# A hybrid diffusion block on one core: retention norm without a mean, states decayed on GpSimd, tiles reordered

## The chip, the cores and the metric

The kernel runs on one core of one Trainium2 chip. The metric is the device time of one execution in microseconds (us). Its engines are TensorE (PE; its weight loads are PEld), VectorE (DVE), ScalarE (ACT), GpSimd (POOL) and SyncE (SP), each with an instruction queue of its own that it works through in order; 16 DMA engines move data.

## The reference

One layer over 1024 latent tokens and 256 context tokens, model width 1024, four gated-DeltaNet heads and four retention heads of 128. What the change touches is the retention group: `r_f` and `r_b` are chunkwise retentions in the two directions, with a state R that is decayed by a constant of the head and chunk, and the norm of their sum subtracts the mean of each head.

```python
def head_group_norm(t, g):
    mu = jnp.mean(t, axis=-1, keepdims=True)
    var = jnp.mean(jnp.square(t - mu), axis=-1, keepdims=True)
    return (t - mu) * lax.rsqrt(var + NORM_EPS) * g.astype(jnp.float32)
...
    def step(S, xs):                      # gated delta rule, per chunk
        u_c, w_c, q_c, qk_c, k_c, gl = xs
        v_new = u_c - jnp.einsum('bhck,bhkv->bhcv', w_c, S)
        o = jnp.einsum('bhck,bhkv->bhcv', q_c, S) + jnp.einsum('bhij,bhjv->bhiv', qk_c, v_new)
        S = gl * S + jnp.einsum('bhck,bhcv->bhkv', k_c, v_new)
        return S, o
...
    def step(R, xs):                      # retention, per chunk
        q_c, k_c, v_c = xs
        o = jnp.einsum('bhik,bhkv->bhiv', q_c * xi[..., None], R)
        R = g_chunk * R + jnp.einsum('bhjk,bhjv->bhkv', k_c * zeta[..., None], v_c)
        return R, o
...
    o_ret = head_group_norm(r_f + r_b, ret_norm_g) * jax.nn.silu(rg...)
    y = jnp.concatenate([o_gdn, o_ret], axis=-1)
    x = x + g1 * (y[:, CTX_LEN:] @ w_out)
```

The output of a retention head is linear in v, and v = h @ w_v: a mean over the 128 columns of a head's output is zero if the mean over these columns has been taken out of the value weights.

## The kernel before

The kernel is written as one program, and a list scheduler decides the order of the instructions on each engine; within an engine they run in that order. A tile of tokens has 128 rows; there are ten, two of context (0, 1) and eight of latent tokens (`LAT`). The span falls into stages:

- To about 86 us: adaLN and the norm. `xt` are loaded token tiles, `junk` their squares, `rx2s`, `rx3s` the square roots of two groups of tiles (four latent ones, two context ones), `xtr` the transposes on TensorE, and `hhi`, `hlo` the modulated result as a high and a low part (L233 to L236).
- Projections. `token_major` (L326) multiplies 128 tokens by 256 columns of weights, in 24 matmuls into a PSUM tile `tm` (L335 to L337); a finishing instruction writes `res`, which goes to DRAM (`rd` for the groups rv, rk, rq, rg, `zd` for z). `fin_copy` (L357) is a Copy on ScalarE, `fin_gate` (L360) a Silu. Weights are split in a high part on ScalarE (`whi`, L279) and a low part (`wlo`, L280). Groups 0 and 1 are rv, 2 and 3 rk, 4 and 5 rq, 6 and 7 rg. The convolutions for k, q and v stand between them.
- The chunk solve of the delta rule, to about 620 us.
- The scan, to 726 us: `step` (L737) in both directions side by side, a state `S` each, with products `kS`, `Tr`, `up`, `o`; beside it the backward retention states `Rb` (`backward`, by `rstate`, L857), for which `kz` is made on GpSimd from a loaded `pk`. `gate` (L796) norms and gates the delta output `O` into `yo`, with `zg` loaded for it.
- Retention, forward (`forward`, L884), with its last four steps from 722 to 762 us: `rqT`, `rkT` (transposes), `qk` (copies on ScalarE and two products with the decays `XI`), `rP` (the product of k and q), `pm` (masked, on VectorE), `ro` (the output), then the norm and the gate, and `ru` for the next state `Rf`. All of `rqT`, `rkT`, `rP`, `ro`, `ru` share the PSUM banks of `bank_a`.
- Output projection (`op`): tiles of y are loaded in the order `pairs` (L1072), transposed (`yT`, L1003), split (`yhi`, `ylo`) and multiplied by `wohi`, `wolo`, which come from `woraw`. Then the FFN and its output (`ffn`, `fo`), to the end.

Square roots of the norms are taken in `rsqrt_mean`: a Sqrt on ScalarE and four or five small instructions on VectorE (`rrx` to `rry` for retention, `rgs` to `rgy` for the delta norm).

## Time and profile before

| | us |
|---|---|
| median of three runs | 1544.87 (1543.34 to 1545.88) |
| the profiled execution, its time | 1540.2 |
| the profiled execution, its span | 1538.3 |
| PE busy | 1440.2 (94%) |
| DVE busy | 988.5 (64%) |
| ACT busy | 621.9 (40%) |
| POOL busy | 644.0 (42%) |

The rows further down come from the profiled execution. Its span begins with its first instruction; start times are counted from there. The granted clock of a stretch is the mean over it, 1.00 for 2.4 GHz and 0.50 for 1.2 GHz.

### The profile page before, as it was taken

The page shows a single profiled execution, that of the slowest core. Times are in us where ns is not written, and L with a number is a line of the kernel's source. Part 1 is how long each engine was busy: PE and PEld are TensorE (multiplying, and loading weights), DVE is VectorE, ACT ScalarE, POOL GpSimd, SP SyncE. Part 2 cuts the span into 40 slices and gives each one's busy share as a digit, 9 for nine tenths or more (in the row PEclk, how much of TensorE's full clock was granted, in tenths as well). Part 3 has the DMA queues.
Part 4 walks back from the last instruction along what each step waited for, and adds up shares of the span by engine and source line. Part 5 has one row for each costly group of instructions (what it writes and reads, how often), then busy time and mean ns, then how long its engine had stood idle before and what let it go on. Part 6 is the DMA issues. An engine that isn't in the chain of part 4 may idle for free.

```text
span 1538.3 us, 24370 instructions
## 1 busy us (share of the span) xinstructions
PE 1440.2 (94%) x8973; PEld 1247.3 (81%) x8973; DVE 988.5 (64%) x1945; ACT 621.9 (40%) x1277; POOL 644.0 (42%) x594
## 2 busy tenths in 40 slices
PE   4799999988989999999799899996999999999997
PEld 1698887987989899999678688875888888888886
DVE  5855679389766634778847776753555555658477
ACT  5743455456451111334534443222333333355444
POOL 2310001476113332224407669987555554226321
PEclk9899999999989999999899999998999999999999
DMA  7554577587585565996743247576222221585862
GB/s 269 188 200 144 155 231 228 159 253 241 165 239 150 176 201 179 354 399 207 260 149 117 110 151 241 204 258 227 103 103 103 103 105 73 190 308 187 291 221 110
DMA packets 156486, 298.15 MB, mean 194 GB/s; under 512 B 43384, under 2 KB 75464, under 8 KB 150992
## 3 DMA queue, kind: packets, MB, share of 16 engines
q1 hardware_dynamic: 116624, 246.88, 47.5%
q10 hardware_dynamic: 36944, 41.08, 8.4%
q0 software_dynamic: 2800, 8.65, 1.6%
q8 instruction: 70, 1.15, 0.3%
q14 instruction: 48, 0.39, 0.1%
HBM read 206.60 MB, written 89.96 MB: 193 GB/s over the span
## 4 chain that ended last, share of the span: by engine, by line
PE 55%; POOL 8%; DMA 8%; DVE 7%; issue 3%; ACT 3%; SPq 0%; ACTq 0%; POOLq 0%; DVEq 0%
PE ffn L1158 6%; PE ffn L1156 6%; PE ffn L1157 6%; PE fo L1281 4%; PE fo L1283 4%; PE fo L1282 4%; PE tm L336 3%; PE tm L337 3%; PE tm L335 3%; DMA wd<-tw 2%; PE op L1018 1%; PE op L1017 1%; PE op L1019 1%; DMA sd<-sp 1%; POOL e L567 1%
## 5 line engine op out<-in xcount | busy, mean ns | idle before, releaser
L336 PE MATMUL tm<-wlo,hhi 128*128 128x256 f32 x704 | 205.8, 294 | 4.9 <-DVE wlo L280 4.9
L335 PE MATMUL tm<-whi,hhi 128*128 128x256 f32 x704 | 203.5, 293 | 5.4 <-ACT whi L279 3.0
L337 PE MATMUL tm<-whi,hlo 128*128 128x256 f32 x704 | 204.3, 293 | 0.0
L336 PEld LDWEIGHTS tm<-wlo,hhi 128*128 128x128 f32 x704 | 139.4, 198 | 7.6 <-DVE wlo L280 5.9
L335 PEld LDWEIGHTS tm<-whi,hhi 128*128 128x128 f32 x704 | 138.1, 198 | 7.6 <-ACT whi L279 3.7
L337 PEld LDWEIGHTS tm<-whi,hlo 128*128 128x128 f32 x704 | 139.2, 199 | 0.5 <-POOL hlo L236 0.2
L1156 PE MATMUL ffn<-t,whi 128*128 128x512 f32 x352 | 136.7, 389 | 1.1 <-ACT whi L279 1.1
L1158 PE MATMUL ffn<-t,wlo 128*128 128x512 f32 x352 | 136.9, 390 | 0.4 <-DVE wlo L280 0.4
L1157 PE MATMUL ffn<-t,whi 128*128 128x512 f32 x352 | 137.0, 389 | 0.0
L279 ACT ACTIVATE whi<-wraw 128x512 fp32r<-128x512 f32 (+1 forms) x98 | 75.2, 772 | 129.3 <-PE ffn L1157 84.5
L279 ACT ACTIVATE whi<-ws 128x512 fp32r<-128x512 f32 x88 | 55.6, 632 | 169.8 <-PE ffn L1157 134.8
L280 DVE TENSOR_TENSOR wlo<-ws,whi 128x512 fp32r<-128x512 f32 x88 | 91.4, 1039 | 46.5 <-ACT whi L279 46.4
L1156 PE MATMUL ffn<-b,whi 128*128 128x512 f32 x264 | 104.8, 397 | 16.5 <-ACT whi L279 16.5
L1282 PE MATMUL fo<-wlo,ahi 128*128 128x512 f32 x308 | 119.8, 389 | 0.0
L1281 PE MATMUL fo<-whi,ahi 128*128 128x512 f32 x308 | 119.3, 389 | 0.1
L1283 PE MATMUL fo<-whi,alo 128*128 128x512 f32 x308 | 119.0, 389 | 0.0
L280 DVE TENSOR_TENSOR wlo<-wraw,whi 128x512 fp32r<-128x512 f32 (+1 forms) x92 | 99.0, 1078 | 20.0 <-ACT whi L279 20.0
L1158 PE MATMUL ffn<-b,wlo 128*128 128x512 f32 x264 | 104.6, 396 | 1.9 <-DVE wlo L280 1.9
L1157 PE MATMUL ffn<-b,whi 128*128 128x512 f32 x264 | 104.6, 396 | 0.0
L280 DVE TENSOR_TENSOR wlo<-raw,whi 128x512 fp32r<-128x512 f32 x77 | 66.6, 890 | 52.1 <-ACT whi L279 52.1
L460 PE MATMUL b<-hhi,whi 128*128 128x512 f32 (+1 forms) x256 | 94.3, 368 | 0.3 <-ACT y L464 0.3
L461 PE MATMUL b<-hlo,whi 128*128 128x512 f32 (+1 forms) x256 | 94.1, 368 | 0.0
(430 smaller groups left out, 3638.1 us busy)
## 6 DMA issues: line engine op xcount, KB each, us to landing
adaw<-ada_w SPq DMA_DIRECT2D x48, 512.0 KB, 4.8
pk<-sd SPq DMA_DIRECT2D x16, 1536.0 KB, 7.8
wraw<-wfi SPq DMA_DIRECT2D x44, 512.0 KB, 3.5
ar<-ad SPq DMA_DIRECT2D x33, 512.0 KB, 4.4
w<-wfo SPq DMA_DIRECT2D x22, 512.0 KB, 5.3
wd<-tw SPq DMA_DIRECT2D x11, 1024.0 KB, 4.8
ad<-act SPq DMA_DIRECT2D x20, 512.0 KB, 3.0
raw<-wd SPq DMA_DIRECT2D x20, 512.0 KB, 6.5
```

Source lines behind the costliest of these rows:

```text
L279: S.activation(hi, raw, AF.Copy)
L280: e.tensor_tensor(lo, raw, hi.bitcast(F32), ALU.subtract)
L335: T.matmul(o, hhi[:, k, tsl], whi[:, k % 4, :], start=(k == 0), stop=False)
L336: T.matmul(o, hhi[:, k, tsl], wlo[:, k % 4, :], start=False, stop=False)
L337: T.matmul(o, hlo[:, k, tsl], whi[:, k % 4, :], start=False, stop=(k == KT - 1))
L460: T.matmul(o, whi[:, k, :], hh, start=(k == 0), stop=False)
L1156: T.matmul(o, whi[:, k, :], xhi(xn, slice(0, 4), k), start=(first and k == 0), stop=False, **kw)
L1157: T.matmul(o, whi[:, k, :], xlo(xn, slice(0, 4), k), start=False, stop=False, **kw)
L1158: T.matmul(o, wlo[:, k, :], xhi(xn, slice(0, 4), k), start=False, stop=(k == 3), **kw)
L1281: T.matmul(po[g][i], ahi[:, ts], whi, start=(j == 0 and not kw), stop=False, **kw)
L1282: T.matmul(po[g][i], ahi[:, ts], wlo, start=False, stop=False, **kw)
L1283: T.matmul(po[g][i], alo[:, ts], whi, start=False, stop=(j == FH - 1), **kw)
```

## The change

Six things change.

1. The value weights (groups 0 and 1) are centred on chip by head: the sum over each 128 columns, times -1/128, is added to them. The retention output then has no mean, and the norm needs only its mean square.
2. rg is projected in the place of rv, and rv in that of rg.
3. In `forward` the evacuation of `ro`, `bn_stats`, `bn_aggr`, `nm` and the Identity go; four Squares read `ro` in PSUM and accumulate `ss`, and four scalar_tensor_tensors take `ro` from PSUM, the root and the gate to `oc`. One of the two `XI` products moves from GpSimd to VectorE, which reads `rqT` in PSUM, and the twelve `ro` matmuls go by operand instead of by head.
4. The old states are multiplied by their decay on GpSimd (`aged`), ahead of the product that they are added to; VectorE then adds 512 columns at once.
5. `zg` has two buffers instead of one, in another pool.
6. Tiles go into `op` in another order.

```diff
+            if center:
+                n = shape[0] * shape[1] // P
+                heads = raw.rearrange("p k (h j) -> p (k h) j", j=P)
+                mean = R1.tile([P, n], F32, tag="mean", name="mean")
+                V.tensor_reduce(mean, heads, axis=AX.X, op=ALU.add)
+                V.scalar_tensor_tensor(heads, bc(mean, [P, n, P], 2), -1.0 / P, heads, ALU.mult, ALU.add)
...
-        for g in range(2):
-            token_major(g, ALL, fin_copy, S, W, SY, last_ada)
-            ada_rest(2, g)
+        for g in (6, 7):
+            token_major(g, LAT, fin_gate, S, W, SY, last_ada)
+            ada_rest(2, g % 2)
...
-        for g in (6, 7):
-            token_major(g, LAT, fin_gate, S, W2, SY)
+        for g in range(2):
+            token_major(g, ALL, fin_copy, S, W2, SY)
...
+            aged = None
+            if old is not None and not last and RTS:
+                aged = RTS[0].tile([P, H, P], F32, tag="aged%d" % d, name="aged%d" % d, bufs=1)
+                G.tensor_tensor(aged, old, bc(sm["gl"][:, c8(t, d)], [P, H, P], 2), ALU.mult)
...
+                elif aged is not None:
+                    V.tensor_tensor(ns.rearrange("p h v -> p (h v)"), pu, aged.rearrange("p h v -> p (h v)"), ALU.add)
...
-            zg = load(SC, zd[l], "zg", 1, (P, 512))
+            zg = load(RTS[0], zd[l], "zg", 2, (P, 512))
...
+            if prev is not None:
+                aged = RT.tile([P, H, P], F32, tag="aged", name="aged", bufs=2)
+                G.tensor_tensor(aged, prev, bc(gch[:, 4 * d:4 * d + 4], [P, H, P], 2), ALU.mult)
...
-                for h in range(H):
-                    V.scalar_tensor_tensor(ns[:, h, :], prev[:, h, :], gch[:, 4 * d + h:4 * d + h + 1],
-                                           pu[:, h * P:(h + 1) * P], ALU.mult, ALU.add)
+                V.tensor_tensor(ns.rearrange("p h v -> p (h v)"), pu, aged.rearrange("p h v -> p (h v)"), ALU.add)
...
-                for d in range(2):
-                    G.tensor_tensor(qk[:, 2 + d], qk[:, 0], XI[d], ALU.mult)
+                V.tensor_tensor(qk[:, 2], pq.rearrange("p (h i) -> p h i", i=P), XI[0], ALU.mult)
+                G.tensor_tensor(qk[:, 3], qk[:, 0], XI[1], ALU.mult)
...
+                for h in range(H):
+                    T.matmul(po[:, hsl[h]], qk[:, 2, h, :], cur[:, h, :], start=(h == 0), stop=(h == 0),
+                             skip_group_check=h > 0)
+                for h in range(H):
+                    T.matmul(po[:, hsl[h]], pm[:, h, :], vv[:, hsl[h]], start=False, stop=False, skip_group_check=True)
+                for h in range(H):
+                    T.matmul(po[:, hsl[h]], qk[:, 3, h, :], rb[t][:, h, :], start=False, stop=True,
+                             skip_group_check=True)
...
+                for h in range(H):
+                    S.activation(oc[:, h, :], po[:, h * P:(h + 1) * P], AF.Square, accum_out=ss[:, h:h + 1])
+                rs = rsqrt_mean(RT, ss, H, "rr", P)
...
-                S.activation(oc.rearrange("p h v -> p (h v)"), po, AF.Copy)
...
-                for h in range(H):
-                    V.bn_stats(bst[:, h, :], oc[:, h, :])
-                for h in range(H):
-                    V.bn_aggr(mv[:, h, :], bst[:, h, :])
-                rs = rsqrt_mean(RT, mv[:, :, 1], H, "rr", 1.0)
...
-                for h in range(H):
-                    S.activation(oc[:, h, :], oc[:, h, :], AF.Identity,
-                                 bias=nm_[:, h:h + 1], scale=rs[:, h:h + 1])
-                yf = oc.rearrange("p h v -> p (h v)")
-                G.tensor_tensor(yf, yf, gt, ALU.mult)
+                    V.scalar_tensor_tensor(oc[:, h, :], po[:, hs], rs[:, h:h + 1], gt[:, hs], ALU.mult, ALU.mult)
...
-        pairs = (0, 4, 1, 5, 2, 6, 3, 7)
-        nxt = op_y(0)
+        pairs = (1, 5, 2, 6, 0, 4, 3, 7)
+        nxt = op_y(1)
```

The scheduler moves instructions. The first place is ScalarE at the front, between the squares of the two context tiles and the modulation of the four latent tiles `hhi` (- is before, + the changed kernel; its lines are some numbers higher, so L357 answers to L368 and L342 to L350).

```order
 L247 ACTIVATE junk,ms<-xt 128x1024 x2
-L357 ACTIVATE res<-tm 128x256
+L368 ACT_TABLE_LOAD
+L368 ACTIVATE res<-tm 128x256
+L125 ACT_TABLE_LOAD
 L125 ACTIVATE rx3s<-ms,epsb 128x2
-L357 ACTIVATE res<-tm 128x256
-L342 DMA rd<-res 128x256 x2
+L368 ACT_TABLE_LOAD
+L368 ACTIVATE res<-tm 128x256
+L350 DMA rd<-res 128x256 x2
 L233 ACTIVATE hhi<-xtr,bmix,amix 128x512 x8
```

Three table loads now stand between the squares and `hhi`; two more stand a few rows earlier, one ahead of the two `res` that come before the first DMA `xt<-ctx`, one ahead of `rx2s`, which comes before the second.

The second place is GpSimd in the scan rounds. Before, the twelve `kz` of the backward states stand there without anything between them.

```order
L354 TENSOR_TENSOR res<-ra,res 128x2x64 x2
L342 DMA rd<-res 128x256
L859 TENSOR_TENSOR kz<-pk,Z 128x512 x12
L898 TENSOR_TENSOR qk<-qk,XI_7004 128x512
L898 TENSOR_TENSOR qk<-qk,XI_7005 128x512
```

In the changed kernel `aged` of the backward states (L876, numbered `Rb`) and of the scan states (L764, `S`) stand between them.

```order
L878 TENSOR_TENSOR kz<-pk,Z 128x512 x3
L876 TENSOR_TENSOR aged<-Rf,gch 128x512
L876 TENSOR_TENSOR aged<-Rb_7147,gch 128x512
L764 TENSOR_TENSOR aged_7279<-S_7209,gl 128x512
L876 TENSOR_TENSOR aged<-Rb_7160,gch 128x512
L764 TENSOR_TENSOR aged_7293<-S_7216,gl 128x512
L878 TENSOR_TENSOR kz<-pk,Z 128x512 x3
L876 TENSOR_TENSOR aged<-Rb_7249,gch 128x512
L876 TENSOR_TENSOR aged<-Rb_7262,gch 128x512
L764 TENSOR_TENSOR aged_7394<-S_7324,gl 128x512
L876 TENSOR_TENSOR aged<-Rb_7275,gch 128x512
L764 TENSOR_TENSOR aged_7408<-S_7331,gl 128x512
```

A round now has three `kz`, three or two `aged` of Rb and two of S, in this order.

The third place is VectorE in the last retention steps. Before, a step's rows there are these: statistics of the step ahead, a group of `yo`, the mask `pm`, the root's small instructions, the four state updates in two pieces.

```order
L915 BN_STATS bst<-oc 128x6 x2
L807 SCALAR_TENSOR_TENSOR yo<-O,rgy,zg 128x128 x4
L915 BN_STATS bst<-oc 128x6 x2
L917 BN_AGGR mv<-bst 128x2 x4
L903 TENSOR_TENSOR pm<-rP,M 128x512
L127 TENSOR_SCALAR rrx<-mv 128x4
L132 RECIPROCAL rry<-rrs 128x4
L136 SCALAR_TENSOR_TENSOR rru<-rry,rrx 128x4
L137 TENSOR_TENSOR rru<-rru,rry 128x4
L138 SCALAR_TENSOR_TENSOR rry<-rru,rry 128x4
L869 SCALAR_TENSOR_TENSOR Rf<-Rf,gch,ru 128x128 x3
L920 SCALAR_TENSOR_TENSOR nm<-mv,rry 128x4
```

In the changed kernel the last steps read so; L939 is the gating of `ro` from PSUM, L914 the XI product, L920 is `pm`, L887 the state's add.

```order
L939 SCALAR_TENSOR_TENSOR oc<-ro,rry,pk 128x128 x4
L887 TENSOR_TENSOR Rf<-ru,aged 128x512
L127 TENSOR_SCALAR rrx<-ss 128x4
L132 RECIPROCAL rry<-rrs 128x4
L136 SCALAR_TENSOR_TENSOR rru<-rry,rrx 128x4
L914 TENSOR_TENSOR qk<-rqT,XI_7016 128x512
L137 TENSOR_TENSOR rru<-rru,rry 128x4
L138 SCALAR_TENSOR_TENSOR rry<-rru,rry 128x4
L939 SCALAR_TENSOR_TENSOR oc<-ro,rry,pk 128x128 x4
L920 TENSOR_TENSOR pm<-rP,M 128x512
L887 TENSOR_TENSOR Rf<-ru,aged 128x512
L1001 SCALAR_TENSOR_TENSOR wolo<-hf,gain,wohi 128x512 x3
```

The last `yo` stand ahead of these rows now, and a gating of the step ahead stands between the XI product and `pm`.

## Rows read from the trace of the kernel before

**Rows 1.** Windows: stretch, length, busy PE PEld DVE ACT POOL, clock, DMA share, GB/s.

```profile
84.00:620.00 536.00, 512.41 (x4263) 470.66 (x4262) 343.48 (x736) 210.42 (x481) 150.05 (x234) 0.96 0.64 198
650.00:675.00 25.00, 25.00 (x224) 24.91 (x224) 16.78 (x61) 6.54 (x17) 6.43 (x7) 1.00 1.00 390
722.00:762.20 40.20, 30.45 (x215) 28.62 (x213) 33.53 (x113) 21.89 (x65) 19.48 (x18) 0.87 0.80 275
775.00:800.00 25.00, 22.69 (x103) 17.34 (x102) 12.68 (x20) 8.65 (x14) 0.00 (x0) 1.00 0.34 114
```

**Rows 2.** Timeline of ScalarE: start, length (us), line, form, [idle before <-releaser].

```profile
60.37 0.41 ACTq L186 DMA_DIRECT2D xt<-ctx  x1
...
65.29 1.06 ACT L247 ACTIVATE junk<-xt 128x1024 f32<-128x1024 f32 x1 [0.83 <-DMA xt<-ctx]
...
67.61 2.12 ACT L233 ACTIVATE hhi<-xtr,bmix,amix 128x512 fp32r<-128x512 f32 x3 [0.44 <-PE xtr L258]
```

**Rows 3.** Timeline of TensorE at the front: the two waits for the modulated tiles.

```profile
68.44 0.38 PE L335 MATMUL tm<-whi,hhi 128*128 128x256 f32 x1 [1.09 <-ACT hhi L233]
...
69.91 1.37 PE L258 MATMUL xtr<-ident,xt 128*128 128x128 f32 x8 [0.49 <-DVE hf L235]
```

**Rows 4.** Groups by line on ScalarE, whole span: the table loads of the gate.

```profile
L360 ACT ACT_TABLE_LOAD x8 | 10.3, 1283 | 3.5 <-DMA zd<-res 2.9 <-ACT vt L704 0.4
```

**Rows 5.** Timeline of ScalarE at a table load and the instruction behind it.

```profile
93.55 1.28 ACT L419 ACT_TABLE_LOAD   x1
94.84 0.21 ACT L419 ACTIVATE nA<-alog 128x8 f32<-128x8 f32 x1
```

**Rows 6.** Timeline of GpSimd in the scan rounds: kz, and what it waited for.

```profile
645.43 1.04 POOL L859 TENSOR_TENSOR kz<-pk,Z 128x512 f32<-128x512 f32 x1 [6.36 <-DMA pk<-rd]
...
649.68 1.04 POOL L859 TENSOR_TENSOR kz<-pk,Z 128x512 f32<-128x512 f32 x1 [1.67 <-PE ru L863]
657.58 1.04 POOL L859 TENSOR_TENSOR kz<-pk,Z 128x512 f32<-128x512 f32 x1 [6.86 <-DMA pk<-rd]
```

**Rows 7.** Timeline of VectorE in the same round: the S update.

```profile
654.26 1.12 DVE L778 SCALAR_TENSOR_TENSOR S<-S,gl,up 128x128 f32<-128x128 f32 x4
```

**Rows 8.** Waits of TensorE, 722 to 768: us in total, times, longest us.

```profile
PE ro L909 <- DVE pm L903: 4.1, 3, 2.6
PE rP L901 <- ACT qk L896: 3.9, 3, 2.0
...
PE rqT L893 <- DMA pk<-rd: 0.8, 1, 0.8
```

**Rows 9.** Timeline of VectorE in the tail: what stands ahead of pm.

```profile
725.39 2.93 DVE L807 SCALAR_TENSOR_TENSOR yo<-O,rgy,zg 128x128 f32<-128x128 f32 x4 [1.12 <-DMA zg<-zd]
...
745.54 3.40 DVE L807 SCALAR_TENSOR_TENSOR yo<-O,rgy,zg 128x128 f32<-128x128 f32 x4
...
755.66 2.65 DVE L127 TENSOR_SCALAR rrx<-mv 128x4 f32<-128x4 f32 x1
```

**Rows 10.** Timeline of GpSimd in the tail: the qk products beside them.

```profile
745.92 2.60 POOL L898 TENSOR_TENSOR qk<-qk,XI 128x512 f32<-128x512 f32 x2
...
755.77 2.50 POOL L898 TENSOR_TENSOR qk<-qk,XI 128x512 f32<-128x512 f32 x2
```

**Rows 11.** Groups by line on VectorE, 620 to 765: mean ns of one is the last figure.

```profile
L869 DVE SCALAR_TENSOR_TENSOR Rf<-Rf,gch,ru 128x128 f32<-128x128 f32 x32 | 9.1, 340 | 0.4 <-PE ru L863 0.4
...
L915 DVE BATCH_NORM_STATS2 bst<-oc 128x6 f32<-128x128 f32 x31 | 6.9, 279 | 7.0 <-ACT oc L911 6.9
```

**Rows 12.** Groups by line on ScalarE, 620 to 765: the squares of the gate.

```profile
L802 ACT ACTIVATE yo<-O 128x128 f32<-128x128 f32 x32 | 9.5, 297 | 9.2 <-DVE O L792 6.1 <-DMA dy<-yo 3.0
```

**Rows 13.** Timeline of TensorE: last retention step, its last ro, first op matmul.

```profile
753.60 0.27 PE L893 MATMUL rqT<-ident,pk 128*128 128x128 f32 x1
...
761.73 0.39 PE L909 MATMUL ro<-pk,pm 128*128 128x128 f32 x2
...
766.83 0.80 PE L1017 MATMUL op<-wohi,yhi 128*128 128x512 f32 x1 [3.32 <-ACT yhi L1006]
```

More of the change, by code (lines that the diff above doesn't have):

```diff
@@ L312, in ada_rest, with weights @@
                     V.scalar_tensor_tensor(o, o, 1.0, gffn[:, ks], ALU.add, ALU.mult)
-        def weights(src, shape, e, pl, q=S, after=None):
+        def weights(src, shape, e, pl, q=S, after=None, center=False):
             raw = pl.tile([P] + shape, F32, tag="wraw", name="wraw")
@@ L326, in token_major @@
         def token_major(g, tiles, finish, store, pl, q=S, after=None):
-            w = [weights(ap["wt"][g, :, 4 * kh:4 * kh + 4, :], [4, 256], V, pl, q, after) for kh in range(2)]
+            w = [weights(ap["wt"][g, :, 4 * kh:4 * kh + 4, :], [4, 256], V, pl, q, after, GROUPS[g // 2] == "rv")
+                 for kh in range(2)]
             c0 = (g % 2) * 256
@@ L362, in build @@
         LAT, ALL = list(range(2, TT)), list(range(2, TT)) + [0, 1]
[L363 to L366 removed]
+        for g in (6, 7):
+            token_major(g, LAT, fin_gate, S, W, SY, last_ada)
+            ada_rest(2, g % 2)
+        checkpoint("rg")
         GS = pool("gs", side="right")
@@ L529, in build @@
         checkpoint("q")
-        for g in (6, 7):
-            token_major(g, LAT, fin_gate, S, W2, SY)
-        checkpoint("rg")
+        for g in range(2):
+            token_major(g, ALL, fin_copy, S, W2, SY)
+        checkpoint("rv")
         close(W2)
@@ L737, in build @@
         seen = set()
+        RTS = []
         def step(s, d):
@@ L828, in build @@
         RT = pool("rt")
+        RTS.append(RT)
         rdl = RT.tile([P, 8], F32, tag="rdl", name="rdl")
@@ L904, in forward @@
                 po = bank_a("ro")
+                hsl = [slice(h * P, (h + 1) * P) for h in range(H)]
+                for h in range(H):
[6 more added lines that the diff above has]
+                             skip_group_check=True)
@@ L905, in forward @@
+                oc = RT.tile([P, H, P], F32, tag="oc", name="oc", bufs=2)
+                ss = RT.tile([P, H], F32, tag="ss", name="ss", bufs=2)
+                for h in range(H):
+                    S.activation(oc[:, h, :], po[:, h * P:(h + 1) * P], AF.Square, accum_out=ss[:, h:h + 1])
+                rs = rsqrt_mean(RT, ss, H, "rr", P)
                 for h in range(H):
                     hs = slice(h * P, (h + 1) * P)
-                    T.matmul(po[:, hs], qk[:, 2, h, :], cur[:, h, :], start=True, stop=False)
@@ L908, in forward @@
-                    T.matmul(po[:, hs], qk[:, 3, h, :], rb[t][:, h, :], start=False, stop=False)
-                    T.matmul(po[:, hs], pm[:, h, :], vv[:, hs], start=False, stop=True)
-                oc = RT.tile([P, H, P], F32, tag="oc", name="oc", bufs=2)
-                S.activation(oc.rearrange("p h v -> p (h v)"), po, AF.Copy)
-                bst = RT.tile([P, H, 6], F32, tag="bst", name="bst", bufs=2)
-                mv = RT.tile([P, H, 2], F32, tag="mv", name="mv", bufs=2)
-                for h in range(H):
-                    V.bn_stats(bst[:, h, :], oc[:, h, :])
@@ L916, in forward @@
-                for h in range(H):
-                    V.bn_aggr(mv[:, h, :], bst[:, h, :])
-                rs = rsqrt_mean(RT, mv[:, :, 1], H, "rr", 1.0)
-                nm_ = RT.tile([P, H], F32, tag="nm", name="nm", bufs=2)
-                V.scalar_tensor_tensor(nm_, mv[:, :, 0], -1.0, rs, ALU.mult, ALU.mult)
-                for h in range(H):
-                    S.activation(oc[:, h, :], oc[:, h, :], AF.Identity,
-                                 bias=nm_[:, h:h + 1], scale=rs[:, h:h + 1])
```

3 lines of the change are left out of this document (1 added, 2 removed).

## The prediction

> **What bounds the kernel now.** I read the page's busy times first. TensorE is busy 94% of the span, so only stretches where it waits, or where it runs at its lower clock, can give anything back. The windows [rows 1] sort the stretches: from 84 to 620 us TensorE is busy 512.41 of 536 us; in the scan rounds it is full (25.00 of 25) with a DMA share of 1.00; in the four last retention steps, 722.0 to 762.2, it is busy only 30.45 of 40.2 us at a mean clock of 0.87; from 775 to 800 it still misses 2.3 us. The reader should keep the third row in mind: 9.75 us idle, and 0.13 x 40.2 = 5.2 us lost to the lower of the two clock levels, 15 us together. That is all the tail can return.
>
> Then I read who ends those idle times. In the tail TensorE waits 4.1 us for pm from VectorE and 3.9 us for the copied, transposed k from ScalarE [rows 8]. Ahead of 84 us the only waits that the change meets are 1.09 us for hhi from ScalarE and 0.49 us for hf from VectorE [rows 3].
>
> **The front: rg takes the place of rv.** The matmuls are the same in size, but the tile's finishing instruction on ScalarE turns from Copy into Silu, between Sqrt instructions of the norm. The order of ScalarE in the changed kernel has five table loads here where before has none: two ahead of the second DMA xt<-ctx (before the first res and before rx2s), three more between the second junk square and the eight hhi. One load takes 1283 ns [rows 4]. The second issue goes from 60.37 to 60.37 + 2 x 1.283 = 62.9 us, and its square already waits 0.83 us for that data [rows 2]. Had the two transfers shared the way, the data comes some 1.0 us later; if not, 2.6 us. Behind it stand 3 x 1.283 = 3.85 us. So the first hhi, at 67.61 before, starts 4.85 to 6.4 us later. TensorE has emptied its queue by then (it waits at 68.44 already), and with 512.41 of 536 us busy behind it [rows 1] it has little idle time that could give the delay back. I take **+5.0**. Least is 3.4 (the three loads less the 0.44 us that ScalarE waits before hhi anyway), most 9 (6.4 and one stretch at the lower clock behind the long gap, half of the tail's 5.2).
>
> In that place the row and the Trainium skill differ. In the trace the load at 93.55 us ends at 94.83 and its own instruction, nA, starts at 94.84 [rows 5]: nothing is lost behind the load. The Trainium skill ("ScalarE: Activation LUTs", section "What ACT_TABLE_LOAD costs") puts a drain of about 1380 ns on top of the 1283, about 2.66 us for every switch; by that the front would cost 6.9 us more than the five loads alone, an estimate from that page. I go by the row.
>
> **The middle, 84 to 620.** Four tensor reductions and four scalar_tensor_tensors of 1024 columns are new on VectorE, about 1.3 us each if a column costs what it does elsewhere; VectorE is busy 343.48 of 536 us there, so they fit beside TensorE. If one stood in front of a weight that TensorE waits for, it would cost its length. The v conv and first chunk products change places with projection tiles. TensorE's idle time is 23.6 us in this stretch, ended by chains that keep their length. I take **0**; bounds -4 and +4, a sixth of that idle time each way.
>
> **The scan rounds, 625 to 726.** Of the updates of S and R on VectorE, which went head by head, 56 and 64 instructions become 14 and 16 adds of 512 columns. TensorE is full here, so this frees nothing on the path. What is new is a wait: S and R now need `aged` from GpSimd. In its order a round reads kz, kz, kz, aged (Rb), aged (Rb), aged (S), aged (Rb), aged (S), and behind a late one everything on GpSimd waits. The nearest row for one aged is kz itself, 1.04 us. The first kz starts at 645.43 after a wait of 6.36 us for DMA, the third, held by its second buffer, at 649.68; the first S decay of the round would end at 649.68 + 1.04 + 3 x 1.04 = 653.8. Its S update runs at 654.26 in the trace [rows 6, 7]: 0.4 us to spare. Counted another way, kz to kz of two rounds is 657.58 - 645.43 = 12.15 us, and the eight instructions end 5.29 + 5 x 1.04 = 10.5 us after the first: 1.65 us to spare. DMA is saturated, and zg's two loads now come into this stretch, so a kz 1 us late is likely in some round. I take **+1.0**. Below, 0; above, the 1.5 us that separate the two counts and their like in each of six rounds, 9.
>
> **The retention tail.** What each step loses: on ScalarE the evacuation and four Identity (replaced by four squares with accumulation, as yo has them); on GpSimd one of two XI products and the gating product; on VectorE four bn_stats of 0.279 and the four Rf updates of 0.340 [rows 11]. It gains a qk product, four gatings and one aged. VectorE's sum hardly moves; GpSimd's falls by about 1.5 us a step. More important is what VectorE does in front of pm. Four yo take 2.93 and 3.40 us, and a tiny rrx 2.65 us, and the last two run beside qk products on GpSimd [rows 9, 10]. zg, which the first of them waited 1.12 us for, has two buffers now. In the order of the changed kernel most yo stand earlier, and of GpSimd's two qk products only one is left; the ro matmuls that need neither pm nor Rb come first, and fill TensorE while pm is made.
>
> A step that nothing disturbs is read from the last one: first transpose at 753.60, last ro ending near 762.12 [rows 13], 8.5 us; pm stood there behind rrx and was some 2.0 us late, so 6.5 us. Four such make 26.0. Three of them I charge with 1.8 us for a yo group, a gating group or a wolo group still in front of pm: 31.3. Today it is 40.2, so **-9.0**. Bounds: four clean steps, -14; only half of the two big waits goes and the clock stays low, (4.1 + 3.9) / 2 = -4.
>
> **The start of op.** From the last ro to the first op matmul (762.12 to 766.83, [rows 13]) it is 4.7 us. Now the first yT needs the PSUM bank of the last ro, which the gating frees: four squares of 0.297 [rows 12], 1.2 us; four gatings of 0.340, 1.4; the root's five small instructions between them and then yT and yhi, 2.5 by my estimate; 5.1 us: +0.4. The pairs' order asks for the last gated tiles last, and wo's second half may land sooner: of the 2.3 us missing from 775 to 800 I take 0.9 back. Together **-0.5**; bounds -3 and +1. Behind it, FFN and output stand in the same order.
>
> **Sum**: 5.0 + 0 + 1.0 - 9.0 - 0.5 = -3.5 us. The profiled execution has a span of 1538.3 and a time of 1540.2, 4.7 under the median of 1544.87; its span would be 1534.8, and the median 1544.87 - 3.5 = **1541.4**.
>
> **Rivals.**
> *The tail is wholly cleared and the front half hidden.* For it: nothing but VectorE's queue holds pm. Against: gating now stands in that queue too. -14 + 3.4 + 0 + 0 = -10.6: 1534.3.
> *Given back.* The tail's waits move to other late things (the gating that holds the ro bank, the loads of pk, for which TensorE waited 0.8 us [rows 8]), and it gains 4 only: 5 + 1 - 4 - 0 = +2: 1546.9, no change that can be told. For it: in this tail DMA has a share of 0.80 and VectorE is busy 33.53 of 40.2 us.
> *Slower: the decays on GpSimd set the round.* If S is late by more than the 0.4 to 1.65 us to spare, each round of both scans is longer, since kS of the next needs it. Six rounds by 1.5 us make +9 in place of +1: 1549.4. For it: the small slack and kz's waits of 6.36 and 6.86 us for DMA; against: the rounds' period is DMA's and TensorE's at once.
> *Slower: a switch costs as much again as its load*, because what is ahead has to drain: 5 x 1.283 = +6.4: 1547.8. It decides if the gap behind a load is over about 1.3 us. Against: [rows 5] show none. The Trainium skill's section cited above says nearly this.
>
> **How the numbers follow.** A measurement of this kernel tells no change from about 0.2%, 3.1 us. Forecast 0.36 (its spread puts two thirds below that line, one third within), cleared 0.12, given back 0.26 (0.06 faster, 0.15 same, 0.05 slower), decays 0.22 (0.03 same, 0.19 slower), switches 0.04. Faster 0.24 + 0.12 + 0.06 = 0.42; same 0.12 + 0.15 + 0.03 = 0.30; slower 0.28. The range reaches from the cleared case, 3 us below its centre, to the decays' case, 2.6 above: 1531 to 1552. The forecast's own is 1537 to 1546.
>
> **What would show it.** Front: five table loads between 59 and 73 us and the first hhi near 72.6; if it starts before 71 the step is wrong. Rounds: S updates not preceded by idle time that ends on GpSimd, and TensorE still full. Tail: from the first of the four steps to the last ro about 31 us, TensorE's wait for pm below 2 us. The prediction fails if the scan rounds grow past 12.2 us, or if the middle moves by more than 4 us, since I have no row that fixes it.

## The result: 7 us slower, and the profile after

The changed kernel takes 1548.68 us (median of 20 runs), the kernel before 1540.97 (20 runs); the ratio is 1.0047, with an interval of 1.0031 to 1.0062, so **+7.2 us**. The forecast was -3.5; it stood on a median of three runs, 1544.87, so the changes are compared here and not the times. The profiled execution of after has a span of 1548.9 us. Its page says that TensorE is as full as before and only busy longer (before: 1440.2 us, 94%):

```profile
PE 1450.1 (94%) x8973; PEld 1256.8 (81%) x8973; DVE 977.5 (63%) x1831; ACT 615.2 (40%) x1302; POOL 653.2 (42%) x608
```

To find where the time went I matched the two traces by TensorE's work: each matmul got the duration that its form has in steady flow, and at equal sums of work the difference of the start times is the lag of after. Both traces are single executions.

| stage, in the times of before | lag at its end | the stage's part | forecast |
|---|---|---|---|
| front, to 77.5 | +6.7 | +6.7 | +5.0 |
| middle, to the last projection at 621.8 | +11.8 | +5.1 | 0 |
| scan rounds, to 723.6 | +21.3 | +9.5 | +1.0 |
| last retention steps, to 761.8 | +13.7 | -7.6 | -9.0 |
| op, to 873.9 | +8.9 | -4.8 | -0.5 |
| FFN and output, to the end | +10.2 | +1.3 | 0 |

Not every row of this table is equally sure. Three variants further down that keep the changed kernel's edits behind the projections (no table loads; neither loads nor centring; after without centring) have +9.3 to +9.7 in the rounds and -7.6 in the tail, as here. The middle is another matter: four variants (the rest of the change alone and the mean kept, two runs each) have before's order of TensorE up to the scan, and their last projection tile ends at 618.6, 620.7, 626.8 and 632.4 us, where before has 620.4. A difference of 5.1 us in this stretch is within what executions of one order differ by.

The windows show the same for four stretches with equal marks in the program (the last `tm`, the entry of the tail, the last `ro`, and 60 us behind it). First before, then after; the columns are those of [rows 1], and the first row is the middle.

```profile
84.00:620.20 536.20, 512.61 (x4265) 470.86 (x4264) 343.48 (x736) 210.42 (x481) 150.05 (x234) 0.96 0.64 198
620.20:720.60 100.40, 98.42 (x868) 97.33 (x868) 79.20 (x297) 38.11 (x106) 34.29 (x35) 1.00 0.86 327
720.60:762.20 41.60, 31.85 (x227) 30.02 (x226) 34.93 (x121) 23.13 (x68) 19.48 (x18) 0.88 0.77 265
762.20:822.20 60.00, 54.06 (x246) 42.82 (x245) 35.33 (x84) 25.57 (x47) 16.08 (x13) 0.94 0.42 141
```

After:

```profile
84.00:634.60 550.60, 528.07 (x4341) 486.07 (x4341) 350.92 (x763) 210.51 (x487) 157.71 (x241) 0.95 0.62 193
634.60:742.00 107.40, 100.52 (x846) 99.37 (x845) 71.16 (x212) 37.02 (x128) 53.13 (x54) 0.95 0.86 328
742.00:776.00 34.00, 26.74 (x223) 24.96 (x222) 29.99 (x83) 17.46 (x72) 11.27 (x12) 1.00 0.78 274
776.00:836.00 60.00, 56.65 (x276) 46.76 (x277) 39.55 (x86) 25.50 (x51) 18.91 (x15) 0.97 0.42 141
```

The tail is 7.6 us shorter and at full clock. The rounds, with 2.0 us of idle time before, lose 6.9 us to it and run at 0.95. Rounds and tail together (second and third row) had 11.7 us of idle time and 0.12 x 41.6 = 5.0 us lost to the clock before; they have 14.1 and 0.05 x 107.4 = 5.4 after. So what the tail no longer loses is lost in the rounds ahead of it. In the middle idle time is nearly the same (23.6 and 22.5 us) though the stretch is 14 us longer.

**The front.** The timeline of ScalarE in after answers to [rows 2], that of TensorE (second fence) to [rows 3].

```profile
59.82 1.28 ACT L368 ACT_TABLE_LOAD   x1
...
61.13 0.33 ACTq L186 DMA_DIRECT2D xt<-ctx  x1
...
61.79 1.28 ACT L125 ACT_TABLE_LOAD   x1
...
67.35 1.28 ACT L368 ACT_TABLE_LOAD   x1
68.65 0.38 ACT L368 ACTIVATE res<-tm 128x256 f32<-128x256 f32 x1
69.05 1.28 ACT L125 ACT_TABLE_LOAD   x1
...
70.66 1.28 ACT L368 ACT_TABLE_LOAD   x1
71.95 0.38 ACT L368 ACTIVATE res<-tm 128x256 f32<-128x256 f32 x1
...
72.79 2.12 ACT L233 ACTIVATE hhi<-xtr,bmix,amix 128x512 fp32r<-128x512 f32 x3 [0.46 <-ACT res L368]
```

```profile
73.62 0.58 PE L343 MATMUL tm<-whi,hhi 128*128 128x256 f32 x1 [5.27 <-ACT hhi L233]
```

Five loads stand there, and hhi starts at 72.79 for 67.61 before. Behind the wait of 5.27 us TensorE runs at the lower of its two levels, where before has 1.00 from 68.4 to 78 us:

```profile
73.60:79.00 5.40, 5.38 (x25) 5.38 (x26) 5.33 (x7) 2.86 (x4) 2.55 (x2) 0.50 0.34 102
```

Behind a load the next instruction starts at once (67.35 + 1.28 = 68.63; res at 68.65), which is what decided the rival of the switches against itself; the drain of about 1380 ns of the Trainium skill ("ScalarE: Activation LUTs", section "What ACT_TABLE_LOAD costs") is not seen in these rows.

**The middle.** What TensorE waits for from 330 to 440 us, first before, then after:

```profile
PE vT L701 <- ACT qt L556: 5.0, 1, 5.0
PE kk L549 <- ACT qt L556: 4.0, 1, 4.0
...
```

```profile
PE kk L557 <- DVE ut L587: 5.0, 1, 5.0
PE vT L709 <- ACT vt L712: 4.6, 2, 4.0
PE b L468 <- ACT y L472: 3.9, 2, 2.6
PE tm L343 <- ACT whi L279: 3.0, 2, 2.1
```

Other chains end the waits. All waits of this window sum to 13.7 us before and 16.5 after, while over the whole middle the idle time hardly differs. What differs more is the clock behind them, in the windows from 440 on (before, then after):

```profile
440.00:480.00 40.00, 35.11 (x495) 33.06 (x494) 19.34 (x50) 12.14 (x18) 5.81 (x10) 0.79 0.60 152
480.00:520.00 40.00, 37.55 (x465) 36.19 (x464) 32.66 (x85) 5.51 (x8) 16.28 (x28) 1.00 0.64 188
```

```profile
440.00:480.00 40.00, 36.54 (x492) 34.74 (x490) 28.53 (x73) 10.54 (x17) 1.26 (x1) 0.69 0.61 146
480.00:520.00 40.00, 39.47 (x445) 38.39 (x446) 26.28 (x70) 4.28 (x7) 14.82 (x25) 0.89 0.81 243
520.00:560.00 40.00, 40.00 (x514) 38.47 (x513) 13.80 (x36) 6.25 (x9) 13.97 (x27) 1.00 0.55 191
```

Length times (1 - clock) from 440 to 560 us is 8.4 us before (its third window is at 1.00) and 12.4 + 4.4 = 16.8 after. That the other order makes this difference isn't shown: the four variants with before's order lose 10.0, 10.4, 18.8 and 18.8 us in the same windows. There TensorE works through the chunk solve's matmuls of 32 and 64 columns with projection tiles between them.

**The rounds.** TensorE's waits from 634 to 744 us, then VectorE's timeline in the first of them and TensorE's wait that it makes:

```profile
PE Tr L778 <- DVE r L773: 4.0, 3, 2.8
PE ro L924 <- DVE qk L914: 2.5, 1, 2.5
...
```

```profile
640.87 0.69 DVE L790 TENSOR_TENSOR S<-up,aged 128x512 f32<-128x512 f32 x1
641.48 1.64 DVE L154 SCALAR_TENSOR_TENSOR lga<-lga,lgq 128x8 f32<-128x8 f32 x4
...
643.96 0.87 DVE L860 TENSOR_SCALAR M<-dist,lgs 128x128 f32<-128x128 f32 x4
...
645.28 0.34 DVE L773 SCALAR_TENSOR_TENSOR r<-kS,neG,pk 128x128 f32<-128x128 f32 x1
```

```profile
645.67 0.49 PE L778 MATMUL Tr<-r,pk 128*128 128x128 f32 x2 [2.77 <-DVE r L773]
```

S is not late here. Between S and the `r` of the next round VectorE makes the small constants of retention (`lga`, `M`). The second wait is for the `XI` product that the change moved to VectorE. The decays themselves take what the forecast took for them (1.04 us); VectorE's add of 512 columns takes 0.686.

```profile
L764 POOL TENSOR_TENSOR aged<-S,gl 128x512 f32<-128x512 f32 x14 | 14.5, 1037 | 13.0 <-DVE S L790 4.9 <-DVE rru L136 4.0 <-DVE rgu L137 1.5
```

**The tail.** Of eight `yo` groups the slowest now take 2.89 us (at 696, in the rounds) and 2.73 (at the entry of the tail), and those beside pm 0.61 for two, where 2.93 and 3.40 for four stood in [rows 9]; the waits from 740 to 782 us answer to [rows 8]:

```profile
PE rP L918 <- ACT qk L913: 3.7, 2, 2.2
PE yT L1017 <- DVE oc L939: 3.5, 1, 3.5
PE ro L927 <- DVE pm L920: 1.5, 2, 0.8
...
```

TensorE's wait for pm went from 4.1 to 1.5 us; the wait for the gated tile is the one that the forecast priced at the start of op.

### The profile page after: what moved, and what is told of

It is laid out like the page before. It is cut to its first block, busy times and chain, and to the rows that moved or that the text cites. A ratio compares the mean times of both kernels' runs of the same rounds, so it can differ in the third digit from the quotient of the medians.

```text
span 1548.9 us, 24327 instructions
## 1 busy us (share of the span) xinstructions
PE 1450.1 (94%) x8973; PEld 1256.8 (81%) x8973; DVE 977.5 (63%) x1831; ACT 615.2 (40%) x1302; POOL 653.2 (42%) x608
## 4 chain that ended last, share of the span: by engine, by line
PE 54%; POOL 6%; DMA 6%; DVE 4%; issue 2%; ACT 1%; SPq 0%; POOLq 0%; ACTq 0%; DVEq 0%
PE ffn L1172 6%; PE ffn L1170 6%; PE ffn L1171 6%; PE fo L1297 4%; PE fo L1295 4%; PE fo L1296 4%; PE tm L343 2%; PE tm L344 2%; DMA wd<-tw 2%; PE tm L345 2%; PE op L1031 2%; PE op L1032 2%; PE op L1033 2%; PE Tr L778 1%; PE ru L882 1%
## 5 line engine op out<-in xcount | busy, mean ns | idle before, releaser
L343 PEld LDWEIGHTS tm<-whi,hhi 128*128 128x128 f32 x704 | 139.4, 200 | 10.9 <-ACT hhi L233 5.7
L1170 PE MATMUL ffn<-b,whi 128*128 128x512 f32 x264 | 105.0, 398 | 16.8 <-ACT whi L279 16.8
L478 DVE SCALAR_TENSOR_TENSOR y<-u,cw,y 128x1022 f32<-128x1022 f32 (+3 forms) x80 | 81.5, 1031 | 21.2 <-ACT y L472 20.9
```

Source lines behind the costliest of these rows:

```text
L343: T.matmul(o, hhi[:, k, tsl], whi[:, k % 4, :], start=(k == 0), stop=False)
L1170: T.matmul(o, whi[:, k, :], xhi(xn, slice(0, 4), k), start=(first and k == 0), stop=False, **kw)
```

## The experiments

Ratios are to the kernel before, timed beside the run on the same chip; differences in us are worked out from them. Not all runs were on one chip, and that a ratio is the same on another isn't shown. First came theory A (the front makes the loss: table loads and what follows from the other order of the groups), against B (the decays on GpSimd hold the rounds). Some runs leave out the gate's Silu or the centring, for timing alone.

**Decays back on VectorE.** Both states as before, all else as after.

```diff
-            if old is not None and not last and RTS:
+            if False:
...
-                G.tensor_tensor(aged, prev, bc(gch[:, 4 * d:4 * d + 4], [P, H, P], 2), ALU.mult)
...
+                for h in range(H):
+                    V.scalar_tensor_tensor(ns[:, h, :], prev[:, h, :], gch[:, 4 * d + h:4 * d + h + 1],
```

> The changed kernel with both decays back on VectorE, head by head. Theory A (the order of the projections is to blame: rg first puts table loads in front of hhi, and brings scan steps ahead of the last projection tiles, so that the retention constants are made with too little TensorE work beside them): the time stays within 3 us of the changed kernel's 1548.7, and TensorE still waits over 2 us for r at the first round after the last projection tile. Theory B (my rival: the decays on GpSimd set the round): 7 to 9 us less, about 1541, and the rounds lose their idle time.

Measured: 1.0071 (1.0052 to 1.0091), +10.9 us, no faster than after. In this kernel `r` stands ahead of `M` (638.33 and 640.55 us on VectorE) and the wait of 2.77 us is gone, yet the time isn't better. B falls; A had the time right and expected that wait to stay.

**No table loads at the front.** Both rg groups are finished with Copy, so the gate's Silu is left out.

```diff
-            token_major(g, LAT, fin_gate, S, W, SY, last_ada)
+            token_major(g, LAT, fin_copy, S, W, SY, last_ada)
```

> The changed kernel with a Copy in the place of the Silu for the rg tiles; the gate's Silu is left out. TensorE's order is that of the changed kernel; five table loads at the front go. Theory A: the first hhi is back at about 68 us, and 5 to 8 us go, about 1542; the stall behind the last projection tile stays. Theory B expects the same of the front, and so does not part from A here; a rival to the table loads (the delayed hhi comes from the changed order of the tiles itself): the first hhi stays past 72 us and no time goes.

Measured: 1.0008 (0.9989 to 1.0028). From 1.0047 that is 6.0 us, with intervals that don't meet, for five loads of 1.283 (6.4); two more go at 106 and 148 us, where TensorE had work. hhi starts at 66.71, TensorE waits 2.26 for it in place of 5.27:

```profile
67.54 0.46 PE L343 MATMUL tm<-whi,hhi 128*128 128x256 f32 x1 [2.26 <-ACT hhi L233]
```

**The swap alone.** The kernel before with rg and rv in each other's place, nothing else.

```diff
-        for g in range(2):
-            token_major(g, ALL, fin_copy, S, W, SY, last_ada)
+        for g in (6, 7):
+            token_major(g, LAT, fin_gate, S, W, SY, last_ada)
```

> The kernel before with nothing but rg and rv in swapped places. TensorE's order up to the scan is that of the changed kernel. Theory A: all of the front's 6.6 us and most of the rounds' 9 us are there without any decay on GpSimd: 12 to 17 us over the kernel before, 1553 to 1558, with the tail as before. Theory B: only the front's 5 to 8 us, 1546 to 1549.

Measured: 1.0113 (1.0088 to 1.0139), +17.4 us. The part of the change that looks like a mere reordering costs over twice what the whole change costs. Theory A's time came; of the rounds' 9 us that it expected there, 1.8 show in the lag, and 12.1 lie in the middle.

**rv first again, centred.** After with rv in its old place.

```diff
-        for g in (6, 7):
-            token_major(g, LAT, fin_gate, S, W, SY, last_ada)
+        for g in range(2):
+            token_major(g, ALL, fin_copy, S, W, SY, last_ada)
```

> The changed kernel with rv first again, its weights centred there, and rg behind conv q. Theory A: the front and the stall at the first round go, the tail's gain of 10 us stays: 7 to 12 us under the kernel before, 1529 to 1534, less up to 3 us if centring delays the first weights. Theory B: the rounds' loss of 9 us stays: 1540 to 1543.

Measured: 1.0147 (1.0112 to 1.0182), +22.6 us: a miss in sign. VectorE centres in front of the first token tiles (two of its rows), and TensorE waits for these:

```profile
47.35 1.21 DVE L326 TENSOR_REDUCE mean<-wraw 128x8 f32<-128x1024 f32 x1
...
48.85 1.22 DVE L327 SCALAR_TENSOR_TENSOR wraw<-mean,wraw 128x1024 f32<-128x1024 f32 x1
49.98 1.41 DVE L251 TENSOR_SCALAR xt<-xt,rx1y 128x1024 f32<-128x1024 f32 x2
```

```profile
50.88 1.51 PE L258 MATMUL xtr<-ident,xt 128*128 128x128 f32 x6 [3.90 <-DVE xt L251]
```

So the swap and the centring belong together: against the same kernel without centring (0.9972, further down), centring in rv's old place costs 27 us, more than the swap.

**The decays one by one.** After with S on VectorE, R on GpSimd (first), and with R on VectorE, S on GpSimd (second).

```diff
-            if old is not None and not last and RTS:
+            if False:
```

> The changed kernel with the decay of the scan's S back on VectorE; the retention states are still decayed on GpSimd. Theory C (formed after the first four runs): with S decayed on GpSimd the scheduler ranks r of the next round behind the retention constants in VectorE's order, and TensorE waits for it; the tail's gain needs the decay of Rf on GpSimd. So the wait of over 2 us for r goes, the rounds get 4 to 6 us shorter, the tail stays: 1542 to 1545 where the changed kernel has 1548.7. Theory D (the backward states' decays hold GpSimd up): the wait for r stays, time within 2 us of the changed kernel's.

```diff
-                G.tensor_tensor(aged, prev, bc(gch[:, 4 * d:4 * d + 4], [P, H, P], 2), ALU.mult)
+                for h in range(H):
+                    V.scalar_tensor_tensor(ns[:, h, :], prev[:, h, :], gch[:, 4 * d + h:4 * d + h + 1],
```

> The changed kernel with the decays of the retention states (Rb and Rf) back on VectorE; S is still decayed on GpSimd. Theory C: the wait for r stays at over 2 us and the tail loses 8 to 10 us of its gain: 1555 to 1558. Theory D: the wait goes, the tail stays: 1543 to 1545.

Measured: 1.0026 (1.0001 to 1.0050) and 1.0048 (1.0019 to 1.0076). R on either engine is the same, and both theories of that run missed. S on VectorE is 3 us better, within the intervals, and TensorE's waits for `r` fall from 4.0 to 2.2 us; but another comes up (`rP` for qk, 3.1 us), and from the last projection to the last `ro` it takes 141.3 us in its trace, as in before (141.7) and in after (141.0).

**Roots without Sqrt.** The roots of the last two norm groups by Newton steps on VectorE, which leaves one load of the five; and, second, retention's small constants made ahead of the scan as well.

```diff
+                if gi >= 2:
+                    V.tensor_scalar(ms, ms, 1.0 / D, EPS, ALU.mult, ALU.add)
+                    rstd = rsqrt(P0, ms, n, "rx%d" % gi)
```

> The changed kernel with the inverse roots of the last two norm groups made on VectorE alone, by Newton steps from a shifted integer, so that no Sqrt stands between the Silu instructions: one table load in the place of five. Theory A's part on the front: the first hhi starts within 2 us of the kernel before's 67.6, and 4 to 7 us go: 1542 to 1545. Against it: the scheduler's order of the middle changes too (64.4 projection tiles ahead of the first scan product, 61.6 in the changed kernel, 69 before), which could move the time by 5 us either way.

```diff
-        rdl = RT.tile([P, 8], F32, tag="rdl", name="rdl")
...
+        rdl = C.tile([P, 8], F32, tag="rdl", name="rdl")
...
+        lg = softplus(C, rdl, 8, "lg")
...
         checkpoint("scan0")
```

> As the run before, and the retention's small constants (rdl to lgs) are loaded and worked out ahead of the rk and rq tiles, in the pool of constants, so that the first retention state waits for less. Theory C: front and r's wait are both gone, 9 to 12 us less than the changed kernel, 1537 to 1540, at the level of the kernel before or a little under it. Rival: the wait for r only changes its place: 1542 to 1545.

Measured: 1.0054 (1.0025 to 1.0083) and 1.0010 (0.9985 to 1.0034). In the first the front is gone (lag -2.4 us by the matched work) and the lag at the last projection tile is +5.1: a miss. The second came out where its rival had it, and is the best of those with rg first and its Silu; which of its edits does it, the intervals don't say.

**The rest of the change alone.** rv first and not centred; scan, retention and op as in after. TensorE's order up to the scan is that of before. In the second S is on VectorE too.

```diff
-            w = [weights(ap["wt"][g, :, 4 * kh:4 * kh + 4, :], [4, 256], V, pl, q, after, GROUPS[g // 2] == "rv")
+            w = [weights(ap["wt"][g, :, 4 * kh:4 * kh + 4, :], [4, 256], V, pl, q, after, False)
```

> The changed kernel with rv first and its weights not centred (the centring is left out): all of the edits of the scan, of retention and of op, and up to 600 us the order of the kernel before. Theory E (the loss sits ahead of the scan: table loads at the front, and in the middle the other order that the scheduler gives the chunk solve as soon as the projections' prologue changes; scan, tail and op are 3 to 5 us faster together): front and middle differ by less than 2 us from the kernel before, and the time is 2 to 6 us under it, 1535 to 1539 for a kernel before of 1541. Rival F (the edits of scan and tail lose by themselves, and their stalls behind the last projection tile are as large here): 3 us or more over the kernel before.

> As the run before (centring left out), with the decay of S on VectorE. Theory C's first half: the wait for r behind the constants goes, up to 4 us less than the run before, 1532 to 1538; if the tail needs GpSimd for S too, the same time as the run before.

Measured: 0.9972 (0.9943 to 1.0000) and 0.9957 (0.9928 to 0.9985). Without the front the change gains 4 us, with an interval that reaches zero, and 7 with S on VectorE. The times came as theory E had them; the middle of the first trace did not (a lag of 6.4 us there, with the order of before).

**The mean kept.** The groups as before, the mean in the norm; bn_stats and Identity read `ro` in PSUM, the gate's product stays on GpSimd; S on VectorE, R on GpSimd (in the second run on VectorE), the other edits of after.

```diff
-                    S.activation(oc[:, h, :], po[:, h * P:(h + 1) * P], AF.Square, accum_out=ss[:, h:h + 1])
-                rs = rsqrt_mean(RT, ss, H, "rr", P)
+                    V.bn_stats(bst[:, h, :], po[:, h * P:(h + 1) * P])
...
+                    S.activation(oc[:, h, :], po[:, h * P:(h + 1) * P], AF.Identity,
+                                 bias=nm_[:, h:h + 1], scale=rs[:, h:h + 1])
```

> The kernel before's order of projections and its norm with the mean, but statistics and normalization straight from PSUM, S decayed on VectorE, R on GpSimd, the first XI product on VectorE, two zg buffers and the new pairs. It computes the reference. Theory E: front and middle as before, the tail gains 2 to 6 us: 1535 to 1539, faster than both kernels. Rival: four bn_stats, Identity and GpSimd's product on the way from ro hold the banks, and the tail is as before: 1540 to 1543.

> As the run before with the retention states decayed on VectorE too, so that no decay is on GpSimd. If the tail's gain comes from VectorE's shorter row of adds, 3 to 6 us more than the run before; if it comes from the products in PSUM and the zg buffers, within 2 us of it.

Measured: 0.9966 (0.9941 to 0.9992) and 0.9977 (0.9947 to 1.0006). The first beats both kernels, by 5 and 12 us; the two don't differ beyond their intervals.

**Neither loads nor centring.** As the run without table loads, and the weights not centred.

```diff
-            w = [weights(ap["wt"][g, :, 4 * kh:4 * kh + 4, :], [4, 256], V, pl, q, after, GROUPS[g // 2] == "rv")
+            w = [weights(ap["wt"][g, :, 4 * kh:4 * kh + 4, :], [4, 256], V, pl, q, after, False)
...
-            token_major(g, LAT, fin_gate, S, W, SY, last_ada)
+            token_major(g, LAT, fin_copy, S, W, SY, last_ada)
```

> The run with rg first and Copy in the place of Silu (it was 1.0008 of the kernel before), now without the centring too; both are left out. It parts what the prologue still costs without table loads (1.0008 against the 0.9972 of the run with rv first and no centring). Theory E1, the order of the groups itself costs 5 us in the middle: still 1.000 to 1.002. Theory E2, the centring's work on VectorE between the weights costs them: 0.996 to 0.998.

Measured: 1.0004 (0.9976 to 1.0032), as with centring (1.0008). What is left over the 0.9972 above would be the order of the groups, 5 us; the two intervals overlap, so this is not told from nothing.

**Centred behind the projection.** rv first; the centring subtracts the mean from each finished value tile, S on VectorE.

```diff
-            S.activation(res, o, AF.Copy)
+            V.tensor_reduce(mean, o3, axis=AX.X, op=ALU.add)
+            V.scalar_tensor_tensor(res.rearrange("p (h j) -> p h j", j=P), bc(mean, [P, 2, P], 2), -1.0 / P, o3,
+                                   ALU.mult, ALU.add)
```

> rv first, weights as they are; the mean of each head is taken from v behind the projection (a reduction and one scalar_tensor_tensor on VectorE for each of the 20 tiles, in the place of the Copy), S decayed on VectorE, all other edits of scan, retention and op. It computes the reference. If the loss of the run with centred weights and rv first (1.0147) came from the late first weights and the order that followed, this one keeps most of the 0.9957 of the run without centring: 0.994 to 0.999. If 26 us is the price of any centring on VectorE ahead of the scan, it is at 1.005 or more.

Measured: 0.9982 (0.9954 to 1.0011). Against +22.6 us with the weights centred in the same place, it is the place of that work on VectorE that costs, with the order that follows from it, and not its amount (S on VectorE, the other difference, is worth 2 to 3 us by the pairs above, neither clear of its intervals).

**The order alone, and after without centring.** First the swap in the kernel before with Copy for the gate; second after with the centring left out.

```diff
+        for g in (6, 7):
+            token_major(g, LAT, fin_copy, S, W, SY, last_ada)
...
+        for g in range(2):
+            token_major(g, ALL, fin_copy, S, W2, SY)
```

> The kernel before with rg projected in the place of rv and rv in that of rg, and with Copy in the place of the gate's Silu for the first group, so that no table load comes between the square roots of the front; the gate is then left unsquashed. Nothing else of the change is made. Theory 'order' (the other order of the groups costs by itself, since other projection tiles and conv blocks then stand beside the chunk products between 330 and 520 us): slower by 5 to 11 us, ratio 1.003 to 1.007, and TensorE waits between 330 and 440 us for y of the convs and for vt as in the kernel after. Rival 'loads only' (swapping costs through the table loads alone, all 17 us of it): no change, ratio 0.999 to 1.001.

```diff
-            w = [weights(ap["wt"][g, :, 4 * kh:4 * kh + 4, :], [4, 256], V, pl, q, after, GROUPS[g // 2] == "rv")
+            w = [weights(ap["wt"][g, :, 4 * kh:4 * kh + 4, :], [4, 256], V, pl, q, after, False)
```

> The kernel after with the centring of the value weights left out and nothing else changed; its retention output then keeps its mean in the norm. Theory 'order and loads' (these two make the change's loss; the four reductions and four products on VectorE find room): same as the kernel after, ratio 1.004 to 1.006 against before. Rival 'centring costs' (their 9.8 us on VectorE push the weights of later groups back): faster than after by 3 us or more, ratio below 1.003.

Measured: 1.0079 (1.0051 to 1.0107) and 1.0102 (1.0074 to 1.0131). The order costs 12.2 us by itself, a little more than its theory had, and the loads would be 5.2 more (1.0113, with intervals that overlap). By the matched work the first run is 1.7 us ahead of before at the front and 12.7 behind at the last projection tile: the cost lies in the middle. Its waits from 330 to 440 are those of after (`vT` for vt 5.6, `b` for y 3.7, `whi` 3.0), and its windows:

```profile
440.00:480.00 40.00, 39.50 (x508) 37.58 (x509) 29.43 (x76) 10.18 (x17) 1.80 (x1) 0.65 0.56 136
480.00:520.00 40.00, 38.97 (x511) 37.73 (x509) 23.62 (x65) 2.95 (x5) 12.98 (x24) 0.96 0.81 261
520.00:560.00 40.00, 40.00 (x385) 38.37 (x385) 11.92 (x31) 5.66 (x8) 13.32 (x25) 0.83 0.49 159
```

That is 14.0 + 1.6 + 6.8 = 22.4 us lost to the clock, more than any of the five runs with before's order (8.4 to 18.8), with TensorE no emptier there; ahead of it, from 84 to 440 us, TensorE is idle 24.6 us for 15.4 before. The second run missed both ways: with less work than after it is 8.5 us slower. Parts of this change don't add up. Centring makes the scheduler write another order, so the order of these two runs is not that of after; and the four runs that share it up to 600 us (these two, the swap alone, neither loads nor centring) lie at 1.0079, 1.0102, 1.0113 and 1.0004 on three chips, so the order up to there does not decide the time by itself either.

## Why the prediction was wrong, point by point

**The steps that failed** are two: the tail's gain as a gain of the kernel, and the middle. The forecast is off by 10.7 us. By the ratios of one chain of edits, 4.2 of these lie in scan, retention and op (-4.3, with an interval from -8.8 to 0, for the forecast's 1.0 - 9.0 - 0.5 = -8.5), 5.5 in the middle (from 0.9972 to 1.0008, an interval that just clears zero) and 1.0 in the loads.

The first: the prediction read 15 us of idle time and lower clock in the tail, took **-9.0** of it back, and charged the rounds **+1.0** for the decays alone. Measured are -7.6 and +9.5, +1.9 together for -8.0: idle time and lower clock of the two stages didn't go (14.1 and 5.4 us, 11.7 and 5.0 before), and 6.9 and 5.4 of them stand in the rounds now. The step that it had wrong is to price the tail for itself, while its work and that of the rounds stand in one order. Why the sum stays is open.

The second: "TensorE's idle time is 23.6 us in this stretch, ended by chains that keep their length. I take **0**; bounds -4 and +4". The idle time did stay (22.5 us). The bound left out the time at the lower clock, which 0.96 over 536 us [rows 1] puts at 21 us more, and left out the change of order, though it was in view: "the v conv and first chunk products change places with projection tiles". The order without centring measures +12.2 us in the kernel before, and some 5 (not clear of its intervals) with the change's other edits; for after's own order, centring included, there are the 5.5 us above and the 5.1 of one trace. Whether the lower clock from 440 to 560 us makes them isn't shown. By either number the middle moved past the 4 us at which the prediction said it fails.

**The front** was right in mechanism: five loads, hhi at 72.79 (forecast 72.6). The second issue of `xt` came at 61.13 and not at 62.9, and its square only 0.9 us later than before (66.18 for 65.29), so the two loads ahead of it cost that, and the three behind it their full 3.85. The term, +5.0, measures +6.7 in the profile and 6.0 by the ratios (5.2 in the kernel before). The difference is the stretch at 0.50 behind the wait, 5.4 us long, which the forecast had in its upper bound alone.

**The rounds**, +1.0, measure +9.5 in the profile, outside the bounds of 0 to 9, and not through what they were bounded by: with both decays back on VectorE the kernel is no faster. The waits seen are for `r` behind retention's constants and for the moved product. They come to 6.5 of the 6.9 us of idle time. VectorE waits for `aged` 1.9 us, all of it for Rb and none for S. The sign that was named came up: from first kz to first kz three rounds take 13.6, 11.6 and 13.2 us, two of them past 12.2. How much of the 9.5 is the tail's work drawn forward isn't shown. From the last projection tile to the last `ro` it takes 140 to 142 us in before, in after and in nine of the sixteen variants, and 143 to 149 in the others: in none did the two stages gain what was forecast.

**The tail** taken alone gained 7.6 of the 9.0, by what was forecast: the slow yo groups no longer stand ahead of pm. It took 34.0 us, TensorE's wait for pm is 1.5, and the clock is 1.00. (The working's 26.0 and three times 1.8 make 31.4, not 31.3, and the term -8.8; nothing hangs on it.)

**Op** gained 4.8, not 0.5: busy time in its first 60 us is 2.6 us more than before, at 0.97 for 0.94. The pairs' order can't have all of it. The swapped kernel, with no edit there, takes 108.7 us from its last `ro` to its last op matmul, the order alone 110.1, before 112.1, after 107.2. All variants with the change's op take 104 to 109, so the 4 us that the rest of the change gains are of the size of op's gain, and did not come from the tail, where the forecast had them.

**The rivals.** "Given back" (1546.9) and "the decays set the round" (1549.4) lie near the time, but neither by its mechanism: the tail kept its gain and the rounds gave it back, and the decays aren't the cause. The table switches cost nothing beyond their loads in the rows, and the pair of runs agrees (6.0 of 6.4 us, where this rival has 12.8).

By the ratios the account of after is -4.3 (scan, retention, op) + 4.9 (order, without loads and centring) + 0.6 (centring) + 6.0 (loads) = +7.2, along one chain of runs from before to after; a chain like this adds up by construction. Along another (centring out first) the loads would be 15 us, of which the traces have 3 at the front, so the terms belong to the chain and not to the edits alone. What stays open: how the order costs time in the middle, whether the lower clock between 440 and 560 us is its doing, and why scan and retention together keep their length.

## What to carry to other kernels

Where a scheduler writes the order, an edit to an early stage has to be priced on the stages behind it that it does not touch: take their idle time and their time at the lower clock as the bounds, and time the reordering alone before the rest. A function that moves to another place on ScalarE brings a table load for every turn between the two functions; in front of an empty TensorE the three that nothing hid counted in full here. A wait that goes from one stage has to be looked for in the stage ahead of it before it is counted as gained. When a part of a change gains and another loses, ship the part: the kernel that kept the mean and the old order of groups, with S on VectorE, was 5 us faster than before.

## What the runs showed of the hardware that was not expected

The granted clock of one stretch differs between executions of the same instructions: with TensorE's order of before up to the scan, the run with the rest of the change alone shows

```profile
440.00:480.00 40.00, 38.24 (x450) 36.30 (x451) 17.02 (x41) 9.48 (x15) 5.76 (x10) 0.57 0.57 140
```

where before has 0.79 and the kernel with the mean kept 0.74. Five traces with this order, before among them, lose 8.4 to 18.8 us to the clock from 440 to 560 us, and their last projection tile ends between 618.6 and 632.4 us. A lag read from one profile in this stretch is uncertain by some 10 us, and only the times of many runs tell the cost of an order.
